# Wide experts of a mixture-of-experts layer: from split three-pass products on 128 columns to native float32 products on four column parts

## The chip, the cores and the metric

One core of a Trainium2 chip runs the whole program. The metric is device time in microseconds (us) of one execution; the kernel before has a median of 2572.89 us over 3 runs (2568.57 to 2573.62).

## What is computed

Two transformer blocks on 256 tokens of width 1024, all float32. The first is SwiGLU, an RWKV time mix beside dilated attention, and SwiGLU; the second has two layers, each a mixer (differential attention beside latent attention) and a feed-forward part, dense in the first and a mixture of 8 experts in the second. The mixture:

```python
logits = xt @ w_router
top_v, top_e = lax.top_k(logits, 2)
gates = softmax(top_v)
# per expert e, on the tokens routed to it:
yb = (silu(xb @ w1[e]) * (xb @ w3[e])) @ w2[e]     # 1024 -> 3584 -> 1024
y[token] += yb * gate
e = sigmoid(x @ w_ple_gate) * (p @ w_ple_proj)
x = layernorm(alpha * x + y + e)
```

## The kernel before, in words

Nearly every product of the program is made in three passes (`mm3`, L291 to L295): both operands are split into a high and a low part in the fast format fp32r (`split`, L236; ACT makes the high part at L241, DVE the low part at L242), and high*high, high*low and low*high are added. Weights come as 512 KB pieces of 128x1024 on SP's queue, through a ring of 4 buffers in pool `wp` and, inside `prefetch`, further ones in pool `wd` (DEEP = 12 in the mixture, 16 in all). `wload` (L280) loads and splits, `fload` (L265) only loads.

The mixture (`moe`) ranks the experts by their tokens. Ranks 0 to 3 are "wide": 128 slots, through `ffn`, with split weights on the whole 128x128 array. Ranks 4 to 7 are "narrow": 64 slots, through `ffn64` (L517): unsplit float32 products, where two halves of 64 columns of the array each take a weight group of their own. Wide and narrow alternate: W1, N1, W2, N2, W3, N3, W4, N4. An expert is 14 groups of 256 hidden columns; of every group there are four input pieces and two output pieces, 84 pieces of 512 KB in all. Input products (IN) write `pin`; silu and a multiplication give `h`; two transposes (TR, L444 or L532) turn it, and output products (OUT) add into `acc`, one group behind.

Tokens reach the slots by products with one-hot matrices (`gather`, L1605, on the high and the low part of x), and leave by products with the transposes (`expert` L1637 and L1638, `expert64` L1652), whose results are added to x on DVE (L1620). The gate of each slot is brought to the slots by a product (`slots`, L1592) and applied when `acc` is split (L244, L245). The gather of the next wide and narrow pair and the gated embedding (`ple`) run as steps between the narrow expert's groups (`beside`); the scatter of an expert is put into the next one's first group. [...]

PE runs its program in the written order, which the tile scheduler has fixed when the kernel is built; SP issues its loads in their own order, and each waits for its buffer.

## Time and profile before

| | before |
|---|---|
| median of 3 runs | 2572.89 us |
| the profiled execution, its time | 2564.82 us |
| its span, first to last instruction | 2563.1 us |
| granted TensorE clock, mean | 0.992 |
| PE / DVE / ACT / POOL busy | 96% / 60% / 48% / 5% |
| DMA moved | 607.11 MB, mean 237 GB/s |
| the mixture's experts, first product to last | 1630.15 to 2549.96 us |

The busy shares are averages over stages with different limits: before 1590 us DMA is often half idle, and from there on its slices in the page stand near 400 GB/s. A PE that is busy need not be at its peak, since the ends of products are modelled; how fast it goes is read from the distance between starts.

### The profile page before, as it was taken

The numbers are of one execution on the slowest core, as the hardware profiler recorded it, in microseconds if no ns is written. First come the engines' busy times: TensorE is split into PE (matmuls) and PEld (weight loads), VectorE is DVE, ScalarE is ACT, GpSimd is POOL, SyncE is SP. The second block draws the span as 40 slices with busy tenths as digits, with TensorE's granted clock in tenths as the row PEclk, the third lists the DMA queues.
The fourth block names the chain that finished last, engine by engine and source line by source line (L and its number), as shares of the span: only waits on it lengthen the run. The fifth ranks groups of instructions, "written<-read, shape, count | busy, mean of one in ns | idle before, by whom it ended". The sixth has DMA issues, their size and how long they took to land. (4 is left out here: it accounts for less than half of the span.)

```text
span 2563.1 us, 38967 instructions
## 1 busy us (share of the span) xinstructions
PE 2470.1 (96%) x14373; PEld 1837.3 (72%) x14373; DVE 1540.4 (60%) x2383; ACT 1230.4 (48%) x2024; POOL 124.5 (5%) x161
## 2 busy tenths in 40 slices
PE   8999999999999999999999999999999999999996
PEld 6778888877788897788878877785377357636731
DVE  7656777765555656765556587893188148607821
ACT  5445554444444466534446563682176137405710
POOL 3200101000000000000000001000000000000000
PEclk9999999999999999999999999999999999999999
DMA  7564222125766443565536436799999999999997
GB/s 269 182 182 153 75 75 82 57 94 185 233 187 185 143 161 125 173 225 192 183 109 197 133 131 237 270 364 370 409 398 350 369 409 380 330 403 409 393 362 292
DMA packets 174344, 607.11 MB, mean 237 GB/s; under 512 B 20288, under 2 KB 25153, under 8 KB 173761
## 3 DMA queue, kind: packets, MB, share of 16 engines
q1 hardware_dynamic: 163872, 584.06, 64.0%
q10 hardware_dynamic: 9232, 18.69, 2.3%
q8 instruction: 115, 1.88, 0.3%
q0 software_dynamic: 1040, 1.78, 0.3%
q14 instruction: 85, 0.69, 0.1%
HBM read 600.78 MB, written 3.67 MB: 236 GB/s over the span
## 5 line engine op out<-in xcount | busy, mean ns | idle before, releaser
L242 DVE TENSOR_TENSOR wlo<-wraw,whi 128x1024 fp32r<-128x1024 f32 (+3 forms) x798 | 951.4, 1213 | 412.4 <-ACT whi L241 396.8
L241 ACT CAST whi<-wraw 128x1024 fp32r<-128x1024 f32 (+3 forms) x798 | 798.9, 1024 | 473.7 <-PE pin L295 261.8
L293 PE MATMUL pin<-whi,xh 128*128 128x512 f32 (+3 forms) x1088 | 409.9, 377 | 6.1 <-ACT whi L241 1.8
L294 PE MATMUL pin<-wlo,xh 128*128 128x512 f32 (+3 forms) x1088 | 406.7, 374 | 4.6 <-DVE wlo L242 4.6
L295 PE MATMUL pin<-whi,xl 128*128 128x512 f32 (+3 forms) x1088 | 406.5, 374 | 3.4 <-DVE xl L242 3.3
L555 PE MATMUL pin<-wraw,xgn 128*64 128x512 f32 x896 | 244.2, 601 | 4.0 <-DMA wraw<-e_in 4.0
L293 PEld LDWEIGHTS pin<-whi,xh 128*128 128x128 f32 x1088 | 206.9, 190 | 45.4 <-issue 8.0
L295 PEld LDWEIGHTS pin<-whi,xl 128*128 128x128 f32 x1088 | 206.7, 190 | 40.7 <-issue 4.9
L294 PEld LDWEIGHTS pin<-wlo,xh 128*128 128x128 f32 x1088 | 207.1, 190 | 39.5 <-DVE wlo L242 6.6
L294 PE MATMUL pin<-wlo,xgh 128*128 128x512 f32 x448 | 183.3, 409 | 1.8 <-DVE wlo L242 1.5
L293 PE MATMUL pin<-whi,xgh 128*128 128x512 f32 x448 | 176.9, 396 | 5.2 <-ACT whi L241 5.2
L295 PE MATMUL pin<-whi,xgl 128*128 128x512 f32 x448 | 175.6, 392 | 0.0
L295 PE MATMUL acc<-whi,hl 128*128 128x512 f32 x422 | 166.7, 396 | 1.0 <-DVE hl L242 0.9
L294 PE MATMUL acc<-wlo,hh 128*128 128x512 f32 x422 | 167.2, 396 | 0.0
L555 PEld LDWEIGHTS pin<-wraw,xgn 128*64 128x64 f32 x896 | 67.9, 136 | 135.9 <-issue 105.0
L293 PE MATMUL acc<-whi,hh 128*128 128x512 f32 x422 | 155.8, 398 | 1.4 <-ACT hh L241 1.4
L293 PE MATMUL pin<-xh,whi 128*128 128x256 f32 x448 | 131.8, 294 | 0.0
L294 PE MATMUL pin<-xl,whi 128*128 128x256 f32 x448 | 130.4, 291 | 0.0
L295 PE MATMUL pin<-xh,wlo 128*128 128x256 f32 x448 | 129.0, 288 | 0.0
L561 DVE TENSOR_TENSOR h<-pin,sg 128x256 f32<-128x256 f32 x28 | 11.9, 424 | 187.5 <-ACT sg L559 187.5
L542 PE MATMUL acc<-wraw,hT 128*64 128x512 f32 x448 | 114.4, 601 | 2.6 <-DMA wraw<-e_out 1.0
L294 PEld LDWEIGHTS pin<-wlo,xgh 128*128 128x128 f32 x448 | 84.3, 188 | 33.1 <-DVE wlo L242 16.0
(537 smaller groups left out, 3617.3 us busy)
## 6 DMA issues: line engine op xcount, KB each, us to landing
wraw<-e_in SPq DMA_DIRECT2D x448, 512.0 KB, 8.8
wraw<-e_out SPq DMA_DIRECT2D x224, 512.0 KB, 9.5
wraw<-ffn_in SPq DMA_DIRECT2D x88, 512.0 KB, 4.7
wraw<-ffn_out SPq DMA_DIRECT2D x44, 512.0 KB, 4.5
wraw<-d_in SPq DMA_DIRECT2D x44, 512.0 KB, 3.7
wraw<-l_dqk SPq DMA_DIRECT2D x32, 512.0 KB, 4.3
wraw<-l_gate SPq DMA_DIRECT2D x32, 512.0 KB, 3.6
wraw<-m_rkv SPq DMA_DIRECT2D x24, 512.0 KB, 3.9
```

The source lines that it names most:

```text
L241: nc.scalar.copy(hi, src)
L242: nc.vector.tensor_sub(lo, src, hi.bitcast(F32))
L293: mm(out, lh, rh, start=start, stop=False, skip_group_check=True)
L294: mm(out, lh, rl, start=False, stop=False, skip_group_check=True)
L295: mm(out, ll, rh, start=False, stop=stop, skip_group_check=True)
L542: mm(acc[R[hf]], t[:, k2, R[g]], w[:, 512 * hf:512 * hf + 512], start=d == 0 and g == 0 and k2 == 0, stop=d == NG // 2 - 1 and g == 1 and ...
L555: mm(out[R[g]], xg[:, kc], w[g][:, 512 * k:512 * k + 512], start=kc == 0, stop=kc == 7, **f)
L561: nc.vector.tensor_mul(hs[d], pin[:, 1], sg)
```

## The change

The narrow scheme becomes one function, `ffn_cols(xg, C, R, ...)`: C column parts of 128/C columns, R blocks of 128/C slots. Narrow is C=2, R=1 as before. Wide is C=4, R=3: 96 slots in three blocks of 32; each of four column parts of 32 takes 256 of the 1024 values of a step (two weight groups, half of each). Weights of the wide experts are no longer split, nor are the gathered tokens, which are written as float32 from one accumulation of the high and the low part. The capacity of wide falls to 96 (no expert has more here, so the branch for overflow stays untaken). Gates are applied at the tokens, when the scattered result is added. The ring of stream buffers grows from 16 to 18; both pools of the stream are allocated from the other end of memory (`side="right"`). The half of x that was multiplied by the residual factor in the first scatter is now multiplied on POOL ahead. The steps beside an expert are: scatter of the expert before, gather and one-hots of the next pair, gated embedding.

```diff
-RAW, DEEP, DEEPF = 4, 12, 6
+RAW, DEEP, DEEPF = 4, 14, 6
-        self.wp = ctx.enter_context(tc.tile_pool(name="wp", bufs=4))
+        self.wp = ctx.enter_context(tc.tile_pool(name="wp", bufs=4, side="right"))
-        with self.tc.tile_pool(name="wd", reuse_waits="tile", bufs=1) as self.deep:
+        with self.tc.tile_pool(name="wd", reuse_waits="tile", bufs=1, side="right") as self.deep:
-    def ffn64(self, xg, NG, win, wout, fill):
+    def ffn_cols(self, xg, C, R, NG, win, wout, fill=None):
...
+        W, n = 128 // C, 1024 // C
+        nh, per = n // 2, 512 // n
+        nt = nh // 128
+        P = [slice(W * c, W * c + W) for c in range(C)]
+        banks = [range(b, min(b + per, R)) for b in range(0, R, per)]
+        acc = [self.acc([len(b), n]) for b in banks]
...
+                    w = self.fload(wout(2 * d + g), 1024 * k)
+                    i, u = (k, g) if C == 2 else (0, 2 * g + k)
+                    for r in range(R):
+                        for c in range(C):
+                            mm(acc[r // per][P[c], r % per], t[:, r * nt + i, P[u]], w[:, n * c:n * c + n],
+                               start=d + g + k == 0 and r % per == 0, stop=d == NG // 2 - 1 and g + k == 2, **f)
...
                     w = [self.fload(win(2 * d + g, half), 1024 * p) for g in range(2)]
                     for k in range(2):
                         kc = 4 * half + 2 * p + k
-                        for g in range(2):
-                            mm(out[R[g]], xg[:, kc], w[g][:, 512 * k:512 * k + 512], start=kc == 0, stop=kc == 7, **f)
+                        v = [x[:, 512 * k:512 * k + 512].rearrange("p (a v c) -> p v a c", a=2, c=nh) for x in w]
+                        for r in range(R):
+                            for c in range(C):
+                                mm(pin[r // per][P[c], r % per].rearrange("p (a c) -> p a c", a=2), xg[:, kc, W * r:W * r + W],
+                                   v[c * 2 // C][:, c % (C // 2)], start=kc == 0 and r % per == 0, stop=kc == 7, **f)
...
+            nc.gpsimd.tensor_scalar(x[:, t, 256 * PLE_A:], x[:, t, 256 * PLE_A:], SQ2, None, op0=ALU.mult)
...
-                for half in range(2):
-                    q = self.pin([512 // n, n])
-                    first = True
-                    for k in range(512 // n):
+                q = self.pin([512 // n, n])
+                first = True
+                for k in range(512 // n):
+                    for part in (xh, xl):
                         for t in range(2):
-                            mm(q[:, k], (xh, xl)[half][:, t, (k0 + k) * 128:(k0 + k + 1) * 128], ohs[:, t], start=first,
+                            mm(q[:, k], part[:, t, (k0 + k) * 128:(k0 + k + 1) * 128], oh[:, t, 0:n], start=first,
                                stop=False, skip_group_check=True)
...
+                nc.scalar.copy(xg[0][:, ks], q[:, :, 0:96])
+                if len(xg) > 1:
+                    nc.vector.tensor_copy(xg[1][:, ks], q[:, :, 128:192])
...
-            acc = self.ffn(xg, 14, win, wout, 1, fill)[0]
-            vh, vl = ep.tile([128, D], F32R, name="vh"), ep.tile([128, D], F32R, name="vl")
-            for h, s in enumerate(H):
-                self.split(vh[:, s], vl[:, s], acc[h], gs)
+            acc = self.ffn_cols(xg, C, R, 14, win, wout, fill)
...
+            for t in range(2):
+                for c0 in range(0, C, 2):
+                    q = [self.pin([n]) for c in range(2)]
+                    for r in range(R):
+                        for i in range(2):
+                            for c in range(2):
+                                p = slice(W * (c0 + c), W * (c0 + c) + W)
+                                mm(q[c], ohT[p, r, t * 128:t * 128 + 128], v[i][p, r], start=r + i == 0, stop=r == R - 1 and i == 1)
+                    for c in range(2):
+                        s = slice(n * (c0 + c), n * (c0 + c) + n)
+                        nc.vector.scalar_tensor_tensor(y[:, t, s], q[c], gate[t], y[:, t, s], op0=ALU.mult, op1=ALU.add)
                     yield
```

**Order on PE, from the gather into the first wide expert.** `oh` holds the one-hot matrices, `gxh` and `gxl` the split tokens, `whi` and `wlo` the split weights, `wraw` a weight piece as loaded, `xg` the gathered tokens, `c` constants with the identity. Before:

```order
L1605 MATMUL pin<-oh,gxh 128x256 x4
L1605 MATMUL pin<-oh,gxl 128x256 x4
...
L1588 MATMUL pin<-c,oh 128x128 x2
L1592 MATMUL pin<-gatr,oh 128x1 x2
...
L293 MATMUL pin<-whi,xgh 128x512
L294 MATMUL pin<-wlo,xgh 128x512
L295 MATMUL pin<-whi,xgl 128x512
```

In the changed kernel:

```order
L1617 MATMUL pin<-oh,gxh 128x256 x2
L1617 MATMUL pin<-oh,gxl 128x256 x2
L564 MATMUL pin<-wraw_15982,xg_15923 32x256 x2
L564 MATMUL pin<-wraw_15984,xg_15923 32x256 x2
...
L1604 MATMUL pin<-c,oh_15973 128x128 x4
L564 MATMUL pin<-wraw,xg_15923 32x256 x48
L537 MATMUL pt<-c,h_16094 128x128 x3
...
L549 MATMUL acc<-wraw_16240,hT_16171 32x256 x12
L549 MATMUL acc<-wraw_16254,hT_16171 32x256 x12
```

The gather alternates high and low part inside one accumulation, the transposes of the one-hots (L1604) have moved behind the first 48 wide products and the gate products are gone; the wide products are 32 columns of the array by 256 values, four to a step, in runs of 96 for IN and 48 for OUT.

**Order on PE, at the start of the first narrow expert.** `vh` and `vl` are the split result of the wide expert, `ohT` the transposed one-hots, `hT` and `hh`, `hl` the turned hidden values. Before:

```order
L444 MATMUL pt<-c,h 128x128 x2
L555 MATMUL pin<-wraw_17194,xgn 64x512
...
L555 MATMUL pin<-wraw_17196,xgn 64x512
L555 MATMUL pin<-wraw_17194,xgn 64x512
...
L1637 MATMUL pin<-vh,ohT 128x512
L1638 MATMUL pin<-vl,ohT 128x512
```

In the changed kernel:

```order
L564 MATMUL pin<-wraw_17302,xg_15924 64x512
L549 MATMUL acc<-wraw,hT_17219 32x256 x48
L564 MATMUL pin<-wraw_17304,xg_15924 64x512
L564 MATMUL pin<-wraw_17302,xg_15924 64x512
...
L564 MATMUL pin<-wraw_17326,xg_15924 64x512
L564 MATMUL pin<-wraw_17328,xg_15924 64x512
L1661 MATMUL pin<-vh_17277,ohT_15974 128x256 x2
L1661 MATMUL pin<-vl_17278,ohT_15974 128x256 x2
```

In both, one narrow product stands alone ahead of the wide expert's last output products; the scatter of the wide expert, 8 products of 512 before, is 48 of 256 now.

**Order on SP, at the loads of the first block's last matrices.** `m_gate`, `m_pr` and `m_wo` belong to the mixer, `ffn_in` to the SwiGLU behind it. Before:

```order
L280 DMA wraw<-m_gate 128x1024 x8
L280 DMA wraw<-m_pr 128x1024 x8
L280 DMA wraw<-m_wo 128x1024 x8
L280 DMA wraw<-ffn_in 128x1024 x2
```

In the changed kernel:

```order
L280 DMA wraw<-m_gate 128x1024 x6
L280 DMA wraw_7391<-ffn_in 128x1024
L280 DMA wraw<-m_gate 128x1024 x2
L280 DMA wraw_7397<-ffn_in 128x1024
L280 DMA wraw<-m_pr 128x1024 x2
L280 DMA wraw_7428<-ffn_in 128x1024
```

Pieces of the second SwiGLU are issued ahead of the mixer's last matrices (six in all).

## Rows read from the trace of the kernel before

**Rows 1.** The page, part 1: busy time, share of the span, instructions.

```profile
PE 2470.1 (96%) x14373; PEld 1837.3 (72%) x14373; DVE 1540.4 (60%) x2383; ACT 1230.4 (48%) x2024; POOL 124.5 (5%) x161
```

**Rows 2.** Windows, one per expert: length; PE, PEld, DVE, ACT, POOL; clock; DMA, GB/s.

```profile
1630.00:1747.00 117.00, 117.00 (x523) 95.00 (x522) 106.34 (x112) 92.74 (x109) 0.00 (x0) 1.00 0.94 345
1747.00:1855.00 108.00, 105.67 (x475) 42.28 (x474) 16.12 (x34) 14.64 (x33) 0.00 (x0) 1.00 1.00 392
1855.00:1980.00 125.00, 123.46 (x533) 95.58 (x534) 110.33 (x117) 89.62 (x112) 0.00 (x0) 1.00 1.00 380
1980.00:2092.00 112.00, 107.76 (x470) 41.63 (x468) 15.39 (x29) 14.46 (x32) 0.00 (x0) 1.00 0.98 378
2092.00:2217.00 125.00, 123.57 (x533) 95.56 (x534) 110.29 (x117) 89.53 (x112) 0.00 (x0) 1.00 1.00 378
2217.00:2321.00 104.00, 99.15 (x410) 33.75 (x408) 11.04 (x24) 11.48 (x29) 0.00 (x0) 1.00 0.98 377
2321.00:2445.00 124.00, 122.91 (x532) 95.39 (x532) 110.07 (x116) 89.47 (x111) 0.00 (x0) 1.00 1.01 395
2445.00:2550.00 105.00, 97.84 (x376) 29.22 (x374) 9.39 (x17) 7.35 (x17) 0.00 (x0) 1.00 0.92 356
```

**Rows 3.** Timeline of PE, last wide products around N1's first: start, length, engine, line.

```profile
1747.00 1.07 PE L555 MATMUL pin<-wraw,xgn 128*64 128x512 f32 x2
1748.01 0.50 PE L293 MATMUL acc<-whi,hh 128*128 128x512 f32 x1
1748.34 0.39 PE L294 MATMUL acc<-wlo,hh 128*128 128x512 f32 x1
...
1750.67 0.39 PE L295 MATMUL acc<-whi,hl 128*128 128x512 f32 x1
1750.99 1.51 PE L555 MATMUL pin<-wraw,xgn 128*64 128x512 f32 x6
```

**Rows 4.** Timeline of PE, end of N1 and start of W2.

```profile
1849.73 4.03 PE L542 MATMUL acc<-wraw,hT 128*64 128x512 f32 x18
1855.49 0.49 PE L293 MATMUL pin<-whi,xgh 128*128 128x512 f32 x1 [1.72 <-ACT whi L241]
```

**Rows 5.** Windows of 10 us: deep in W2, deep in N1, early in N2.

```profile
1900.00:1910.00 10.00, 10.00 (x45) 7.90 (x44) 8.46 (x11) 7.72 (x11) 0.00 (x0) 1.00 1.03 406
1800.00:1810.00 10.00, 10.00 (x46) 3.77 (x45) 0.44 (x2) 0.75 (x3) 0.00 (x0) 1.00 1.03 410
1990.00:2000.00 10.00, 9.07 (x37) 3.61 (x37) 2.79 (x6) 1.39 (x4) 0.00 (x0) 1.00 0.85 294
```

**Rows 6.** Groups by line in W2 (1856 to 1980): busy, mean ns, idle before.

```profile
L242 DVE TENSOR_TENSOR wlo<-wraw,whi 128x1024 fp32r<-128x1024 f32 x84 | 98.2, 1220 | 12.8 <-ACT whi L241 12.8
L241 ACT CAST whi<-wraw 128x1024 fp32r<-128x1024 f32 x83 | 81.6, 1048 | 1.2 <-PE pin L295 1.2
L444 PE MATMUL pt<-c,h 128*128 128x128 f32 x28 | 5.3, 272 | 0.0
```

**Rows 7.** Timeline of PE, products of 256 ahead of the gather, and the gather.

```profile
1616.98 0.28 PE L295 MATMUL pin<-whi,xl 128*128 128x256 f32 x1
...
1622.38 0.28 PE L295 MATMUL pin<-whi,xl 128*128 128x256 f32 x1
1622.49 0.64 PE L1605 MATMUL pin<-oh,gxh 128*128 128x256 f32 x4
1623.44 0.71 PE L1605 MATMUL pin<-oh,gxl 128*128 128x256 f32 x4 [0.31 <-ACT plt L1449]
...
1630.15 0.48 PE L293 MATMUL pin<-whi,xgh 128*128 128x512 f32 x1
```

**Rows 8.** Timeline of PE, first layer's embedding, waits for split weights.

```profile
1117.58 0.38 PE L293 MATMUL pin<-whi,pTh 128*128 128x256 f32 x1 [1.55 <-ACT whi L241]
1118.93 0.58 PE L294 MATMUL pin<-wlo,pTh 128*128 128x256 f32 x1 [0.97 <-DVE wlo L242]
```

**Rows 9.** Windows of 2 us in the RWKV stage.

```profile
300.00:302.00 2.00, 2.00 (x57) 1.91 (x56) 1.34 (x4) 0.36 (x2) 0.00 (x0) 1.00 0.77 197
```

## The prediction

> **What bounds the kernel now.** I read the page's busy times first: PE is busy 96% of the span, DVE 60%, ACT 48% [rows 1]. That is an average, so next I cut the mixture into one window per expert [rows 2]. The reader is to see two kinds of window alternating. In the wide ones PE is busy almost throughout (123.46 of 125 us in W2), and DVE (110 us) and ACT (90 us) split weights beside it; in the narrow ones DVE and ACT do almost nothing and the loads run at 377 to 392 GB/s. The ceiling of the loads shows in single slices: 410 GB/s at share 1.03 deep in N1, 406 deep in W2, while just after a wide expert only 294 [rows 5]. At 409 GB/s a piece of 512 KB takes 1.28 us, and an expert of 84 pieces 107.7 us. Narrow windows are 104 to 112 us long, so loads set their length; the wide ones are 117 to 125 us, some 9 to 17 us above the load time, so what bounds them is PE. The change acts on just that.

> How fast PE goes is read from starts. In the wide tail, ten products of 512 columns start between 1748.34 and 1750.67: 0.233 us each [rows 3]. A narrow run of 18 rows, that is nine pairs of a pass on either half of the array, lasts 4.03 us, the last row 0.60: (4.03 - 0.60) / 8 = 0.429 us for a pair [rows 4]. [...]

> **The change, part by part.** *Wide products.* Before, a wide expert has 14 groups x (8 IN + 4 OUT) x 3 passes = 504 products of 512: 504 x 0.233 = 117.4 us. Now it has 7 x 96 IN and 7 x 48 OUT products = 1008, each two passes of 256 columns; if four column parts run side by side as two do, 2016 / 4 = 504 steps of half the narrow pair, 0.2147 us: 108.2 us. That is 9.2 us less for each wide expert. No row shows four parts that each take all 128 rows, so the step is the open price of this prediction. Its bounds are 0.2147 us, no loss, and 0.429 us, when only the two streams seen in [rows 4] are served at once. I take 0.2147, the nearest row's: adding the second part cost nothing there. Issuing is no obstacle: a step needs four passes with their weight loads in 0.2147 us, 0.054 us for one, and in the RWKV stage 57 products with loads went in 2 us, 0.035 us for one [rows 9].

> *Transposes and visits.* 28 transposes [rows 6] become 21. Theirs are products of 128 columns, so at most the 0.12 us that 256 columns take in [rows 7]: -0.8 us. But float32 column parts and whole-array work now alternate in the wide expert. A change of mode has a price in [rows 3]: the lone narrow product ends its two passes 0.86 us after 1747.00 but the next starts 1.01 after it (0.15 late), the following after 0.33 instead of 0.233 (0.10), and the narrow run after 0.32 (0.09): 0.34 us a visit. A wide expert gets 7 such visits for its transposes and about 4 more for scatter or one-hots: 11 x 0.34 = +3.7 us. Bounds: 0, where the run hides it, and 1 us a visit, which is the whole lone product's time.

> *Scatter of the wide expert.* 8 products of 512 (8 x 0.233 = 1.9 us) become 48 of 256 columns on 32 rows. A row of 256 costs (1622.38 - 1616.98) / 45 = 0.12 us [rows 7]; two row parts at a time make 2.9 us, one after another 5.8. I take 2.9, +1.0 us; the other end is +3.9. It is also cut into four steps beside the narrow expert's groups, where it was one; I charge two more visits, +0.7. That one narrow product stands alone ahead of the last output products is so before and after, 0.

> Sum for a wide expert: -9.2 - 0.8 + 3.7 + 1.0 + 0.7 = -4.6 us; four times, **-18**, rounded. The 1.72 us for which the next wide expert waits for split weights [rows 4] I leave standing: with no split the first product waits for nothing but its piece, yet narrow work queued ahead of it ends later by about as much. If it does go, three times -1.7 are -5.

> *Splitting.* 84 DVE splits of 98.2 us and 83 ACT splits of 81.6 us go from each wide expert [rows 6]. They lie beside PE, which waited for them next to nowhere, so they earn nothing; what ends late in their place is the load. Gates at the tokens (eight DVE operations of 256 columns for four of 512) and the factor on POOL cost nothing: DVE is then nearly idle, POOL is idle (0.00 in [rows 2]), and the first scatter that reads POOL's result is a whole expert away.

> *Lead-in.* From the gather's first product at 1622.49 to the first expert's at 1630.15 are 7.66 us [rows 7]. 32 products at 0.12 are 3.8; the rest is waiting for `pin` to be emptied between the halves, one-hot transposes and gate products, which are now removed or behind the first wide products: **-4**, bounds -1 (only the gate products) and -6.

> *Earlier stages.* The pools at the other end of memory let pieces be issued earlier. In the order on SP six pieces move ahead of the mixer's matrices; what they displace can bear it, for the loads average 237 GB/s over the span, against the 410 of [rows 5]. The clearest cover is the first layer's embedding, where PE stood 1.55 and 0.97 us for split weights [rows 8]: **-2.5**, bounds 0 and -5. Deeper buffers (18 for 16) move SP ahead by two pieces only; in N1 and W2 the loads run at their ceiling anyway, 0.

> Sum: -18 - 4 - 2.5 = -24.5. The profiled execution took 2564.8 us, 1.7 more than its span, so 2540.3 for one like it; the median of the runs is 8.1 us above, and by the same difference I forecast 2572.9 - 24.5 = **2548 us**.

> **The rivals.** *Four parts do not get four streams (slower).* The decisive number is the step: there are 4 x 504 = 2016, so the 24.5 us are used up when a step costs 24.5 / 2016 = 0.012 more, at 0.227 us. That is a loss of 6% beside two parts. If only two parts are served, a wide expert takes 504 x 0.429, 108 us more each: 2548 + 433 = 2981. If four parts do the work of three, 0.286 us: 2548 + 144 = 2692. For it: no row has four such parts. Against it: the pairs of [rows 4] lose nothing, and 57 products in 2 us [rows 9] show that PE follows several tiles in order. Chance 0.07 for two streams, 0.06 for three of four, 0.11 for a smaller loss of 0.230 to 0.26 us (2579 to 2640). [...]

> *Loads become the bound everywhere.* If visits and scatter hide and four parts run freely, each expert falls to the load time: the windows of [rows 2] add up to 920 us, 8 x 107.7 = 862, so up to -58: 2515. Against it: PE's own work in a wide expert stays above 108.2 us, and loads pause at the changes of expert even now (294 GB/s [rows 5]). Chance 0.07.

> *The gain is lost in small pieces.* Steps of 0.225 to 0.230 us, or visits of 0.8 to 1 us, end at 2568 to 2578. Chance 0.08, which is "same"; slower by visits and scatter alone (1 us a visit and the scatter's other end: 29 + 12 = 41, then 2589) 0.02.

> **How the numbers follow.** The forecast's own case, faster, has 0.59, and with the load-bound one faster has 0.66; same 0.08; slower 0.07 + 0.06 + 0.11 + 0.02 = 0.26. Within 0.2%, 5 us, a measurement cannot tell it from no change. The range leaves out two streams (0.07), three of four (0.06) and the lowest end of the load-bound case, so it runs from 2520 to 2640; the likeliest case alone would be 2530 to 2566, by the ends of the lead-in (-2, +3), the early stages (2.5 either way), the wait for split weights (-5), the visits (down to 0: -16, of which I take half) and steps up to 0.221 us (+13).

> **What the changed profile would show.** Right: in the wide expert PE rows of 32 array columns by 256, about 180 in 10 us of a clean stretch (4 / 0.2147 us); wide windows near 120 us, narrow ones unchanged; ACT and DVE below 10 us per wide window; the gather's products done by about 4 us after its first. Wrong: rows of the four parts starting two by two, 0.43 us apart; wide windows over 125 us; or PE idle between steps, waiting for pieces or for its own instructions, of which a wide expert now has twice as many.

## The result, and the profile after

The changed kernel takes 2525.91 us (median of 4 runs, 2524.29 to 2529.44); the kernel before, timed beside it, 2571.55 (4 runs, 2568.57 to 2573.62). The ratio is 0.9825, with a 95% interval of 0.9808 to 0.9842: 45.6 us less, where 24.5 were forecast. The time lies inside the range of 2520 to 2640, 22 us under the forecast and 4 us under the likeliest case of 2530 to 2566. The two profiled executions differ by less, 2563.1 to 2527.7 us in span, because that of before (2564.82) was 7 us under its median and that of after (2529.44) 3.5 over its own.

Part 1 of the page of after, and two of its groups:

```profile
PE 2445.9 (97%) x20537; PEld 1739.7 (69%) x20537; DVE 1123.1 (44%) x1991; ACT 894.9 (35%) x1652; POOL 127.1 (5%) x167
...
L242 DVE TENSOR_TENSOR wlo<-wraw,whi 128x1024 fp32r<-128x1024 f32 (+3 forms) x462 | 554.7, 1205 | 371.0 <-ACT whi L241 360.7
...
L564 PE MATMUL pin<-wraw,xg 128*32 128x256 f32 (+1 forms) x6272 | 557.0, 411 | 2.3 <-DMA wraw<-e_in 2.3
```

Against [rows 1], DVE has lost 417 us and ACT 335, PE's busy time 24. The input products of the experts (L564, wide and narrow) waited 2.3 us in all for their pieces. The windows of after, one per expert, in the columns of [rows 2]:

```profile
1622.00:1732.00 110.00, 109.54 (x1949) 64.11 (x1948) 6.33 (x21) 10.63 (x26) 0.00 (x0) 1.00 0.96 363
1732.00:1841.00 109.00, 107.97 (x601) 44.63 (x603) 14.00 (x31) 12.56 (x30) 0.00 (x0) 1.00 1.02 405
1841.00:1961.00 120.00, 119.03 (x2047) 72.75 (x2043) 8.62 (x21) 8.71 (x23) 0.00 (x0) 1.00 1.02 403
1961.00:2072.00 111.00, 109.75 (x500) 42.23 (x502) 13.91 (x31) 11.59 (x29) 0.00 (x0) 1.00 0.99 382
2072.00:2192.00 120.00, 119.03 (x2045) 72.79 (x2041) 8.79 (x21) 8.71 (x23) 0.00 (x0) 1.00 1.02 394
2192.00:2292.00 100.00, 99.39 (x442) 34.88 (x438) 8.75 (x21) 8.55 (x24) 0.00 (x0) 1.00 0.99 381
2292.00:2412.00 120.00, 119.35 (x2047) 72.92 (x2045) 7.99 (x19) 8.82 (x23) 0.00 (x0) 1.00 1.03 407
2412.00:2515.00 103.00, 97.43 (x410) 30.36 (x406) 10.37 (x22) 6.54 (x17) 0.00 (x0) 0.99 0.94 369
```

From first product to first product, the wide experts went from 116.9, 124.2, 124.3 and 124.2 us to 110.3, 120.3, 120.3 and 120.0 (-18.5 in sum), the narrow ones from 108.5, 112.7, 104.4 and 104.7 to 108.2, 110.9, 100.0 and 102.9 (-8.4). Among its signs the forecast had the narrow ones as unchanged; in its sum each was charged 1.7 us more. PE is now busy nearly all through N1 to N3 too (109.75 of 111, 99.39 of 100), so waiting for loads no longer sets their length.

The step of four parts shows in three neighbouring runs of W2 (timeline of PE in after):

```profile
1867.46 5.36 PE L549 MATMUL acc<-wraw,hT 128*32 128x256 f32 x96
1872.64 5.39 PE L564 MATMUL pin<-wraw,xg 128*32 128x256 f32 x96
1877.96 0.55 PE L537 MATMUL pt<-c,h 128*128 128x128 f32 x3
```

A run of 96 rows is 24 steps of four passes (a pass is a row of the trace, and a product of unsplit float32 is two: the 4 x 1008 products of the wide experts are 8064 rows), and from its start to the next run's are 1872.64 - 1867.46 = 5.18 us: **0.2158 us a step**, against the 0.2147 forecast and the 0.227 at which the gain would have been gone. The mean over 1811 unbroken steps of all four wide experts is the same 0.2158. The transposes stand between 1877.96 and the next products at 1878.43.

The lead-in, from the gather's first product to the first expert's (timeline of PE in after):

```profile
1618.17 0.40 PE L1617 MATMUL pin<-oh,gxh 128*128 128x256 f32 x2
...
1621.74 0.40 PE L1617 MATMUL pin<-oh,gxl 128*128 128x256 f32 x2
1622.07 1.50 PE L564 MATMUL pin<-wraw,xg 128*32 128x256 f32 x24
```

It is 3.90 us instead of the 7.66 of [rows 7].

### The profile page after: what moved, and what is told of

Its sections match the earlier page's. It is cut to its first block, busy times and chain, and to the rows that moved or that the text cites. A ratio compares the mean times of both kernels' runs of the same rounds, so it can differ in the third digit from the quotient of the medians.

```text
span 2527.7 us, 49959 instructions
## 1 busy us (share of the span) xinstructions
PE 2445.9 (97%) x20537; PEld 1739.7 (69%) x20537; DVE 1123.1 (44%) x1991; ACT 894.9 (35%) x1652; POOL 127.1 (5%) x167
## 5 line engine op out<-in xcount | busy, mean ns | idle before, releaser
L242 DVE TENSOR_TENSOR wlo<-wraw,whi 128x1024 fp32r<-128x1024 f32 (+3 forms) x462 | 554.7, 1205 | 371.0 <-ACT whi L241 360.7
L241 ACT CAST whi<-wraw 128x1024 fp32r<-128x1024 f32 (+3 forms) x462 | 464.5, 1008 | 457.4 <-PE pin L295 225.8
L564 PE MATMUL pin<-wraw,xg 128*32 128x256 f32 (+1 forms) x6272 | 557.0, 411 | 2.3 <-DMA wraw<-e_in 2.3
L564 PEld LDWEIGHTS pin<-wraw,xg 128*32 128x32 f32 (+1 forms) x6272 | 253.0, 113 | 241.1 <-issue 113.5
L549 PE MATMUL acc<-wraw,hT 128*32 128x256 f32 (+1 forms) x3136 | 282.6, 411 | 3.2 <-ACT hT L539 1.7
L549 PEld LDWEIGHTS acc<-wraw,hT 128*32 128x32 f32 (+1 forms) x3136 | 124.8, 113 | 109.3 <-issue 39.8
L294 PEld LDWEIGHTS pin<-xl,whi 128*128 128x128 f32 x448 | 86.3, 193 | 1.6 <-issue 0.3
L295 PEld LDWEIGHTS pin<-xh,wlo 128*128 128x128 f32 x448 | 86.4, 193 | 0.7
L293 PEld LDWEIGHTS pin<-xh,whi 128*128 128x128 f32 x448 | 86.3, 193 | 0.7
L295 PE MATMUL acc<-whi,hl 128*128 128x512 f32 x198 | 77.5, 392 | 1.0 <-DVE hl L242 0.9
```

Source lines behind the costliest of these rows:

```text
L241: nc.scalar.copy(hi, src)
L242: nc.vector.tensor_sub(lo, src, hi.bitcast(F32))
L293: mm(out, lh, rh, start=start, stop=False, skip_group_check=True)
L294: mm(out, lh, rl, start=False, stop=False, skip_group_check=True)
L295: mm(out, ll, rh, start=False, stop=stop, skip_group_check=True)
L549: mm(acc[r // per][P[c], r % per], t[:, r * nt + i, P[u]], w[:, n * c:n * c + n], start=d + g + k == 0 and r % per == 0, stop=d == NG // 2 ...
```

## The experiments

Two theories stood first. One: all of the gain is the wide arithmetic, and the unforeseen part comes from its effect on loads and waits. The rival: the deeper ring or the place of the pools, charged with nothing and 2.5 us, bring the unforeseen part. The first three runs undo one part of the change each, beside runs of the kernel before at 2569.8 us.

**Wide experts on split weights again.** The rest of the change stays, with the ring of 16, since two more buffers don't fit beside the split tokens:

```diff
-RAW, DEEP, DEEPF = 4, 14, 6
+RAW, DEEP, DEEPF = 4, 12, 6
...
+            acc = self.ffn(xg, 14, win, wout, 1, fill and (lambda j: fill(j, 0)))[0]
+            for h, s in enumerate(H):
+                self.split(vh[:, s], vl[:, s], acc[h])
...
+                    mm(q, o, vh[:, s], start=True, stop=False)
+                    mm(q, o, vl[:, s], start=False, stop=True)
+                    nc.vector.scalar_tensor_tensor(y[:, t, s], q, gate[t], y[:, t, s], op0=ALU.mult, op1=ALU.add)
```

> The changed kernel with the wide experts' products undone: 128 slots, weights split, three passes on the whole array; gates at the tokens, the one accumulation of the gather and the pools' side stay, the ring is 16. If the four column parts carry the gain of the mixture, each wide window goes back to about 124 us, the narrow ones end again with PE waiting for loads, and the time is 2545 to 2555 us. If the gain is that of the stream and of the new order of gather and scatter, wide windows stay near 120 and it is 2528 to 2535.

Measured: 2553.3 us, ratio to before 0.9941 (0.9922 to 0.996). Two of its windows, W2 and W4:

```profile
1840.00:1968.00 128.00, 126.26 (x533) 96.85 (x534) 110.24 (x117) 89.66 (x112) 0.00 (x0) 0.99 1.00 374
...
2304.00:2432.00 128.00, 126.25 (x532) 96.80 (x532) 110.31 (x117) 89.86 (x112) 0.00 (x0) 0.99 1.00 381
```

The mixture takes 919.6 us, as before the change (919.8), and the wait at the start of W2 is back:

```profile
1840.40 0.50 PE L293 MATMUL pin<-whi,xgh 128*128 128x512 f32 x1 [1.63 <-ACT whi L241]
...
1842.25 0.63 PE L295 MATMUL pin<-whi,xgl 128*128 128x512 f32 x1
...
1844.81 0.44 PE L295 MATMUL pin<-whi,xgl 128*128 128x512 f32 x1
```

Two things in these windows are not the products' own. From 1841.5 us on the granted clock is 0.50 of full speed for 3.4 us: the six steps between the last two rows take 0.427 us each instead of 0.232. That costs about 1.5 us, and it happens at the start of W2, W3 and W4 of this execution and in none of before's. The other is the distance between products, which comes up below with the pools. Yet the whole is 16.5 us under before, so that much lies outside the wide products.

**The ring alone.**

```diff
-RAW, DEEP, DEEPF = 4, 14, 6
+RAW, DEEP, DEEPF = 4, 12, 6
```

> The changed kernel with the ring back at 16 buffers. If the two buffers matter only where PE runs out of loads, which the changed profile shows nowhere for long, 2526 to 2531 us. If the ring is what keeps the narrow experts from waiting at their ends, up to 7 us for each narrow expert come back and it is 2540 to 2550.

Measured: 2532.59 us, 0.9852 (0.9836 to 0.9868), between the two forecasts and nearer the first. Against the kernel with split weights, which has the same ring, it is 20.7 us less, 19.1 of them in the mixture (919.6 to 900.5), the drops of the clock included. Against the mixture of the kernel before it is 19.3. The ring of 18 is worth the 6.7 from here to the changed kernel by medians. The interval of the ratio overlaps with that of the changed kernel's repeat (0.982 to 0.9857, below), but the mixture's length shows the step too: 900.5 us here, 892.9 and 892.7 in two executions with 18. Wide windows are alike in both; the narrow ones are 111.3, 111.2, 102.8 and 104.5 here. The end of N3 with 16 buffers:

```profile
2295.24 2.27 PE L549 MATMUL acc<-wraw,hT 128*64 128x512 f32 x8 [0.29 <-DMA wraw<-e_out]
2297.71 1.08 PE L549 MATMUL acc<-wraw,hT 128*64 128x512 f32 x4 [0.20 <-DMA wraw<-e_out]
2298.99 1.08 PE L549 MATMUL acc<-wraw,hT 128*64 128x512 f32 x4 [0.20 <-DMA wraw<-e_out]
2300.27 0.41 PE L564 MATMUL pin<-wraw,xg 128*32 128x256 f32 x2 [0.20 <-DMA wraw<-e_in]
```

and with 18, in the changed kernel:

```profile
2284.41 1.03 PE L549 MATMUL acc<-wraw,hT 128*64 128x512 f32 x4
2285.55 0.44 PE L537 MATMUL pt<-c,h 128*128 128x128 f32 x2
2285.92 6.23 PE L549 MATMUL acc<-wraw,hT 128*64 128x512 f32 x28
2292.08 0.63 PE L564 MATMUL pin<-wraw,xg 128*32 128x256 f32 x4
```

With 16, PE goes from piece to piece and waits for each: the last three rows start 1.28 us apart, the load time of a piece, where four rows take 0.86. With 18 it runs 28 rows through. The reading that fits, argued and not shown by a run of its own: a wide window of 120 us is longer than the load time of 107.7, so SP gets ahead there by as many pieces as there are buffers, and the narrow window uses them up. A kernel before with a ring of 18 was to show the ring by itself (2561 to 2565 us if it feeds the ends of the narrow experts, 2569 to 2573 if not). It gives no time: pool `wd` would need 56 KB a partition, and beside the split weights and tokens 52.7 are left. So what the ring is worth without the native products stays open, and its gain here hangs on the room that they made.

**The place of the pools.**

```diff
-        self.wp = ctx.enter_context(tc.tile_pool(name="wp", bufs=4, side="right"))
+        self.wp = ctx.enter_context(tc.tile_pool(name="wp", bufs=4))
...
-        with self.tc.tile_pool(name="wd", reuse_waits="tile", bufs=1, side="right") as self.deep:
+        with self.tc.tile_pool(name="wd", reuse_waits="tile", bufs=1) as self.deep:
```

> The changed kernel with both pools of the stream back at the first end of memory. If the pools' side gives the earlier start of the stages ahead of the mixture, second SwiGLU, first layer and start of the first expert come 3 to 6 us later, 2529 to 2532 us; if the side does nothing, 2526.

Measured: 2535.59 us, 0.9862 (0.9846 to 0.9879), above both forecasts: the side is worth 9.7 us by medians, and 9.5 or 5.9 by the ratios, with the changed kernel's first measurement or its repeat. The mixture is no slower than that of the changed kernel (889.9 us against 892.9); the difference lies ahead of it. From about 670 us (the second SwiGLU) to the gather it takes 952.0 us, against 940.6 in the changed kernel and 951.1 before.

The second set ran beside before at 2568.78 us. First the changed kernel again, as a yardstick:

> The changed kernel once more, as the base for the kernels beside it on this chip: 2523 to 2530 us. Its first stages, up to the second SwiGLU, are the same instructions as before, so what their length differs by here is chance between executions (5 us in the profiled one).

Measured: 2526.1 us, 0.9839 (0.982 to 0.9857).

**The kernel before, with both pools moved and nothing else.**

```diff
-        self.wp = ctx.enter_context(tc.tile_pool(name="wp", bufs=4))
+        self.wp = ctx.enter_context(tc.tile_pool(name="wp", bufs=4, side="right"))
...
-        with self.tc.tile_pool(name="wd", reuse_waits="tile", bufs=1) as self.deep:
+        with self.tc.tile_pool(name="wd", reuse_waits="tile", bufs=1, side="right") as self.deep:
```

> The kernel before with both pools of the stream at the other end of memory, and nothing else. If the side is what the changed kernel without it lost, the stages from the second SwiGLU to the gather are 8 to 10 us shorter and it is 2560 to 2563 us, with wide and narrow windows as before; if the side pays only with the changed mixture, 2568 to 2571.

Measured: 2552.23 us, 0.9944 (0.9927 to 0.9962), 16.5 us less by medians, 14.4 by the ratio, and below both forecasts. In the profiled executions 12.0 us of it lie between the second SwiGLU and the gather (951.1 to 939.1) and 3.4 in the mixture (919.8 to 916.4). By medians of two sets the way from before to after is: with the pools moved 2552.2, with the rest of the change but split products 2553.3, with native products 2532.6, with the ring of 18 2526. (The second step hides gains and losses: the lead-in is shorter, while the mixture with split products takes 919.6 us, against 916.4 in this kernel, the three drops of the clock among them.)

By what road? The forecast's was earlier loads. In the first layer's embedding, the waits of PE for split weights are nearly those of [rows 8] (timeline of the moved-pool kernel):

```profile
1109.54 0.38 PE L293 MATMUL pin<-whi,pTh 128*128 128x256 f32 x1 [1.53 <-ACT whi L241]
1110.91 0.39 PE L294 MATMUL pin<-wlo,pTh 128*128 128x256 f32 x1 [0.98 <-DVE wlo L242]
1114.70 0.38 PE L294 MATMUL pin<-wlo,xh 128*128 128x256 f32 x1 [0.22 <-DVE wlo L242]
```

1.53 and 0.98, where 1.55 and 0.97 stood. The last row's 0.22 us is what is left of two later waits of before, 1.32 and 0.44 us:

```profile
1124.58 0.39 PE L293 MATMUL pin<-whi,xh 128*128 128x256 f32 x1 [1.32 <-ACT whi L241]
...
1125.84 0.39 PE L294 MATMUL pin<-wlo,xh 128*128 128x256 f32 x1 [0.44 <-DVE wlo L242]
```

That is 1.6 us of the 16.5. (Over all traces PE is idle 27.7 us on average between the second SwiGLU and the gather where `wd` is moved, eight traces of 25.1 to 28.4, and 29.7 where it isn't, six of 27.6 to 31.4: 2 us.) Most of the rest is in the products themselves. The last products of the first layer's mixer follow each other without a gap in every kernel. Before:

```profile
1099.83 0.39 PE L294 MATMUL pin<-wlo,mTh 128*128 128x512 f32 x1
...
1107.06 0.40 PE L295 MATMUL pin<-whi,mTl 128*128 128x512 f32 x1
```

After:

```profile
1104.66 0.39 PE L293 MATMUL pin<-whi,mTh 128*128 128x512 f32 x1
...
1111.69 0.39 PE L294 MATMUL pin<-wlo,mTh 128*128 128x512 f32 x1
```

Between the two rows lie 31 steps in each, parts of the same unbroken run of 87 products: 7.23 / 31 = 0.2332 us before, 7.03 / 31 = 0.2268 after, at a granted clock of 1.00 in both. **A product of the same kind starts 3% sooner here after the one before it, and nothing about it has changed but where its operands lie.** Over all products of 512 columns in this stage it is 1% (230.9 ns to 228.7). The next runs ask what of the place does it.

**One pool alone, and shifts by a few bytes**, beside before at 2572.24 us.

```diff
-        self.wp = ctx.enter_context(tc.tile_pool(name="wp", bufs=4))
+        self.wp = ctx.enter_context(tc.tile_pool(name="wp", bufs=4, side="right"))
```

> The kernel before with only the pool of the split weights (wp) at the other end, the deep ring (wd) where it was. The kernel with both there was 16 us faster, and its fp32r products of 256 columns start 0.116 us apart for 0.119, those of 512 0.229 for 0.231. If the place of the split weights sets that distance, all of it is here: 0.116 and 0.229 us, 2552 to 2556 us. If the gain is of loads that can be issued earlier into the deep ring, the distances are as before and it is 2564 to 2570.

```diff
-        self.nh = self.cp.tile([128, 8], F32, name="nh")
+        self.nh = self.cp.tile([128, 24], F32, name="nh")
```

> The kernel before with one small constant tile made 64 bytes longer, so that every later tile of that end starts 64 bytes further: the split weights then start 96 bytes past a multiple of 128, as they do at the other end (32 before). If that offset sets the distance between products, it falls to 0.116 and 0.229 us as with the other end, 2552 to 2560 us; if it is the region, the distances stay at 0.119 and 0.231, 2566 to 2572.

```diff
-        self.nh = self.cp.tile([128, 8], F32, name="nh")
+        self.nh = self.cp.tile([128, 16], F32, name="nh")
```

> The same with 32 bytes: split weights and tokens both start 64 bytes past a multiple of 128. If the start's offset matters, the distance changes one way or the other by 0.002 us or more for products of 256; if the region matters, 0.119 and 0.231 us, 2566 to 2572.

Last, beside before at 2572.37 us, the pool of the activations instead of that of the weights:

```diff
-        self.xp = ctx.enter_context(tc.tile_pool(name="xp", bufs=1))
+        self.xp = ctx.enter_context(tc.tile_pool(name="xp", bufs=1, side="right"))
```

> The kernel before with the pool of x and its split transposes (xp), not that of the weights, at the other end. If the distance between products hangs on where the split weights lie, it stays at 0.119 and 0.231 us and the time is 2566 to 2574; if it hangs on how weights and tokens lie to each other, or on the tokens, it changes, to 0.116 and 0.229 us and 2558 to 2564 if they need only be apart.

Measured; the pitches are mean distances between starts of neighbouring fp32r products of one size at a granted clock of 1.00, worked out from the starts in each trace (the first layer's mixer, 342 of 256 columns and about 470 of 512; the mixture's three-pass products, about 1800):

| kernel | time, us | ratio (95%) | 256, ns | 512, ns | mixture 512, ns |
|---|---|---|---|---|---|
| before | | | 119.4 | 230.9 | 230.8 |
| both pools moved | 2552.23 | 0.9944 | 115.4 | 228.7 | 228.9 |
| weights' pool `wp` moved | 2560.62 | 0.9968 (0.9955 to 0.998) | 115.8 | 228.8 | 229.0 |
| all shifted by 64 bytes | 2573.39 | 1.0009 (0.9999 to 1.002) | 119.5 | 230.8 | 230.8 |
| all shifted by 32 bytes | 2571.54 | 0.9999 (0.9982 to 1.0016) | 119.4 | 230.8 | 231.5 |
| activations' pool `xp` moved | 2577.44 | 1.0025 (1.001 to 1.004) | 117.8 | 233.3 | 230.8 |
| the change, split products, pools moved | 2553.3 | 0.9941 | 115.6 | 228.8 | 231.7 |
| the change, pools not moved | 2535.59 | 0.9862 | 119.5 | 230.9 | |
| the change | 2525.91 | 0.9825 | 115.1 | 228.8 | |

`wp` holds the split weights, and moving it alone gives the whole drop in pitch. Its time, though, falls between the two forecasts. Small shifts give nothing. With the activations moved, 512 columns are slower (233.3 ns for 230.9) and 256 faster (117.8 for 119.4), which neither branch of its forecast had; the mixture's products, whose tokens aren't in `xp`, stay at 230.8. And with split products in the changed kernel the mixture's pitch is 231.7 ns although `wp` lies where the others have 229: there the tokens' pool holds other tiles. So in these runs the pitch went with the place of more than the weights. A move to the other end changes it in the mixer (230.9 ns at 512 columns to 228.8 with `wp`, 233.3 with `xp`), an offset of 32 or 64 bytes does not (230.8 with either); distances between were not run. Nor was one operand moved by itself: the pools of one end lie behind each other, so that moving `wp` or `xp` should also shift what is opened after it. Whether the place acts by itself or through other engines' traffic there was not separated either. By which rule the pitch follows stays open.

Count times difference, summed over all stages of before, is 13 us (3.4 of it in the mixture's three-pass products, 1803 x 1.9 ns); `wp` alone brought 11.6 by medians, 8.2 by the ratio (5 to 12). Both pools together bring 6 us more by the ratios, whose intervals overlap; earlier loads show about 2 us of that, and the rest is not settled.

**What holds the changed kernel.** Two more runs of the second set. In the first, the third block of 32 slots goes, so PE has a third less wide work:

```diff
-                done = expert((4, 2)[i], (3, 1)[i], xg[i], places[i], *weights(e), fill(work))
+                done = expert((4, 2)[i], (2, 1)[i], xg[i], places[i], *weights(e), fill(work))
```

> The changed kernel with two of the three blocks of 32 slots computed in the wide experts (the third block is left out, so the outputs lack it): a third less PE work, 36 us, in each wide expert, and the same loads. If PE sets the pace of the wide experts, as their windows of 120 us say, they shrink until the loads bind, 107.7 us for an expert, and the mixture's 893 us become about 865: 2495 to 2500. If the loads already set it, 2520 to 2526.

Measured: 2499.68 us, 0.9735 (0.9716 to 0.9755). Three of its windows (W2 to W3) and what PE waited for in the mixture (us, times, longest):

```profile
1827.00:1931.00 104.00, 88.77 (x1368) 44.67 (x1366) 7.62 (x14) 6.25 (x16) 0.00 (x0) 1.00 1.03 408
1931.00:2048.00 117.00, 112.09 (x482) 41.77 (x482) 13.20 (x29) 11.16 (x27) 0.00 (x0) 1.00 1.02 406
2048.00:2152.00 104.00, 88.46 (x1368) 44.78 (x1366) 7.77 (x14) 5.88 (x16) 0.00 (x0) 1.00 1.02 406
```

```profile
PE pin L564 <- DMA wraw<-e_in: 62.7, 139, 1.3
```

Of 145 us of PE work taken away (4 x 168 steps x 0.2158) only 26 come back: from N1 to W4 the loads run at 405 to 409 GB/s and PE's input products wait 62.7 us for them. The mixture takes 867.9 us, the floor that the loads set.

The second keeps all the work and changes only its order on PE. In the changed kernel, narrow products stand alone or in small groups between visits (start of N3):

```profile
2192.09 1.94 PE L564 MATMUL pin<-wraw,xg 128*64 128x512 f32 x8
2193.96 0.38 PE L1661 MATMUL pin<-vh,ohT 32*128 32x256 f32 x2
...
2194.50 1.07 PE L564 MATMUL pin<-wraw,xg 128*64 128x512 f32 x2
2195.50 0.38 PE L1661 MATMUL pin<-vl,ohT 32*128 32x256 f32 x2
...
2196.05 1.93 PE L564 MATMUL pin<-wraw,xg 128*64 128x512 f32 x6
```

Two rows are one product, without a partner on the other half of the array: it holds PE from 2194.50 to 2195.50, 1.0 us, where a pair side by side takes 0.86 ([rows 4]: 2 x 0.429). The edit chains PE's instructions of the mixture in written order and puts the side work next to the transposes:

```diff
+    def link(self, ins):
+        if self.chain is not False:
+            if self.chain is not None:
+                self.tc.add_manual_dep(ins.ins, self.chain.name, mybir.DependencyInfo(
+                    mybir.DependencyClass.NoSync, mybir.DependencyReason.DATA), reason="pe order")
+            self.chain = ins.ins
...
-            if fill:
+            if fill and C == 4:
                 fill(d, 0)
...
                 if half == 0 and d:
                     TR(d - 1)
+                if half == 0 and fill and C == 2:
+                    fill(d, 0)
...
-            if fill:
-                fill(d, 1)
             if d:
                 OUT(d - 1)
+            if fill:
+                fill(d, 1)
```

> The changed kernel with the order on PE pinned to the written one through the mixture, so that scatter, gather and one-hot steps stand together, beside the transposes of the narrow expert, instead of between single narrow products: half the changes of mode, and 4 lone narrow products for 64. If visits and lost partners are what the narrow experts spend over their 72 us of products, PE gets ahead of the loads and the loads bind: 2496 to 2508 us. If the loads bind in the narrow experts already, 2520 to 2527.

Measured: 2506.88 us, 0.9764 (0.9747 to 0.978), 19 us under the changed kernel with the same instructions. N3 begins so (L573 and L1672 are L564 and L1661 of above):

```profile
2169.61 7.09 PE L573 MATMUL pin<-wraw,xg 128*64 128x512 f32 x32
2176.62 0.39 PE L1672 MATMUL pin<-vh,ohT 32*128 32x256 f32 x2
...
2177.66 3.65 PE L573 MATMUL pin<-wraw,xg 128*64 128x512 f32 x16
2181.25 0.44 PE L546 MATMUL pt<-c,h 128*128 128x128 f32 x2
```

```profile
1831.00:1948.00 117.00, 115.71 (x2050) 67.97 (x2048) 8.65 (x20) 8.79 (x23) 0.00 (x0) 1.00 1.03 407
1948.00:2053.00 105.00, 101.94 (x504) 40.63 (x501) 14.12 (x31) 11.80 (x28) 0.00 (x0) 1.00 1.03 408
2053.00:2169.00 116.00, 114.71 (x2038) 67.50 (x2041) 8.64 (x20) 8.58 (x22) 0.00 (x0) 1.00 1.02 403
2169.00:2266.00 97.00, 93.60 (x454) 33.11 (x442) 8.66 (x21) 8.77 (x25) 0.00 (x0) 1.00 1.03 408
```

Runs of products are whole, and the loads are at 403 to 408 GB/s: with 875.9 us for the mixture it has come within 8 us of the floor that the run with two blocks showed. W1 and N4 are longer than in the changed kernel, by 5.7 and 2.4 us; the other six are 2.1 to 6.1 us shorter. The traces bear out the count in the forecast: over the mixture, PE's work falls into 291 runs of one tile shape in the changed kernel, and in 64 of its narrow runs a product has no partner; reordered it is 188 runs and 4. The kernel before has 188 and 56, so the lone products were there already, and the change added the visits. Two more buffers on top (the tokens and one-hots of the wide expert held once instead of twice make the room), with the last set:

```diff
-RAW, DEEP, DEEPF = 4, 14, 6
+RAW, DEEP, DEEPF = 4, 16, 6
...
-            xg = [ep.tile([128, 8, 96], F32, name="xg96", bufs=2), ep.tile([128, 8, 64], F32, name="xg64", bufs=2)][:len(cols)]
+            xg = [ep.tile([128, 8, 96], F32, name="xg96"), ep.tile([128, 8, 64], F32, name="xg64", bufs=2)][:len(cols)]
```

> The changed kernel with PE's order pinned, as in the run that took 2506.9 us, and 20 buffers in the ring, with room from single copies of the wide expert's gathered tokens and one-hots. There the loads ran at 405 to 410 GB/s from 1740 us on, so deeper buffers can only add what is loaded ahead of the first expert: two pieces, 2.6 us, 2502 to 2505 us; if something else than the loads binds, 2506 to 2508.

Measured: 2503.24 us, 0.9736 (0.9705 to 0.9767), with 872.4 us for the mixture. The step from the ring of 18 is within the intervals. Of the versions that leave nothing out it is the fastest, 2.6% under before.

## Why the prediction was right, and where it fell short

**Four parts, four streams: right.** The open price was the step; 0.2147 us was taken, 0.2158 measured. That a second part costs nothing, which the forecast carried over to four, the rows bear out: the two rows of the lone product in [rows 3] hold PE from 1747.00 to 1748.01, 1.01 us, and two pairs in [rows 4] take 2 x 0.429 = 0.86.

**Wide products at -18: the total fits, in part by luck.** With the ring left at 16 the mixture is 19.3 us less. But of the 4.6 us of the sum for a wide expert, +1.7 (scatter and its visits) fall into the narrow expert beside it, so the forecast for the wide windows was -6.3 each, -25.2 for four, and they gave 18.8; the narrow ones were charged +6.8 and gave -0.5. The two errors cancel. The first has a cause: the old product was priced at 0.233 us from ten products of [rows 3], where the mean of 1803 in the mixture is 0.2308. With that and the step of 0.2158 the arithmetic is worth 7.6 us for an expert and not 9.2. W2 to W4 came out 3.9 to 4.2 less (W1 6.5), which leaves about 4.3 for visits there, against 3.7.

**Lead-in: right** on the terms of [rows 7]: -3.8 against -4.

**"Earlier stages ... -2.5": the step that failed most.** Both the size (-6 to -10 in the changed kernel, -14 to -16.5 alone) and the mechanism. The diff's words `side="right"` were read as a matter of when a piece may be issued. The two waits that were named as the clearest cover still stand, at 1.53 and 0.98 us; what changed is the pitch of the fp32r products, which the prediction took as given: some 13 us of the 16.5, with about 2 for earlier loads.

**"Deeper buffers (18 for 16) ... 0": failed.** It argued that loads run at their ceiling anyway. They do inside a narrow window, but not over a pair: 377 to 392 GB/s in N1 to N3 of [rows 2], under the 410 of [rows 5]. With two buffers more the narrow windows are 7.9 us shorter in sum; -6.5 to -6.7 us for the whole by medians.

**The wait of 1.72 us "left standing": failed,** by its own second reading. The prediction had the bound of three times -1.7; in the changed kernel no gap over 0.2 us stands in the 12 us ahead of W2, W3 or W4, and narrow work queued there did not end later by as much. With the wait taken out, the narrow experts' share of the forecast is +6.8 - 5.2 = +1.6, against the -0.5 measured with the ring of 16. Whether the scatter's price was right is not shown by that, since loads still set the end of N3 there.

**Splitting at nothing: borne out.** 417 us less on DVE and 335 on ACT shortened no wide window beyond what PE's own work gave. What they did bring is the wait above and the room for the ring.

**The load-bound rival (2515)** was not reached, though the room was there: the order of PE's visits and lone products kept the time 19 us above what the reordered kernel reaches.

In sum, forecast and measured: wide products -18, and -15.9 (916.4 to 900.5, both with the pools moved; the pitch takes the rest of the 19.3); lead-in -4 and -3.8; pools -2.5 and -16.5, the mixture's share among them; ring 0 and -6.5. These add up to -42.7, the difference of medians in the second set; the first measurement's -45.6 is 3 us more, and the medians of before alone lie between 2568.8 and 2572.4. So the direction was forecast for the right reason, but more than half of the gain came from the two parts priced at 2.5 us and at nothing. That the time still lies inside the range is luck: the range went down to 2520 for the load-bound rival, which is not what happened.

## What to carry to other kernels

Price an edit of where a buffer lies as an edit of speed, not only of order: compare the distance between starts of the same product in the same stage before and after, since the waits and the rows' own lengths (0.39 us in both) don't show it. Where work that is bound by an engine alternates with work that is bound by loads, price the buffers in between by what the first leaves over, even if loads are at their ceiling in the second: two of them were worth 6.7 us here by medians. And on an array that is divided into column parts, count the products that stand without a partner in the final order on PE: here a better order of them and of the visits between them was worth 19 us, more than the 15.9 that the native products gained.

## What the runs showed of the hardware

PE's granted clock drops from 1.00 to 0.50 of full speed for stretches of 3.4 to 16.0 us, nine in the profiled execution of before and eleven in that of after, most of them ahead of the mixture and at other moments in each execution. Up to the second SwiGLU, where before and after have the same instructions, they add up to 17.1 us in the profiled execution of before, 34.4 in that of after and 17.4 in that of its repeat; the second SwiGLU starts at 671.4, 677.6 and 671.6 us.
